# Gate and up projections: seven block products in place of eight for three of eight pairs of K tiles

## The chip, the cores and the metric

The kernel runs on one core of one Trainium2 chip. The metric is the device time of one execution in microseconds (us). TensorE is called PE below, VectorE DVE, ScalarE ACT, GpSimd POOL and SyncE SP; PEld is TensorE's loading of the stationary operand.

## The reference

The program is a two-layer encoder trunk over 256 tokens of width 2048, all in float32. Each layer computes

```
h = x + W_out [ attention | convolution | spatial gating ](RMSNorm(x))
x = h + ( silu(n @ W_gate) * (n @ W_up) ) @ W_down        with n = RMSNorm(h)
```

and a last RMSNorm follows. `W_gate` and `W_up` are 2048 x 5632 in each layer, and `W_down` is 5632 x 2048. The change is in `n @ W_gate` and `n @ W_up`; what the kernel must return is the same.

## The kernel before, in words

**Three matmuls for one float32 product.** Every operand of a large matmul is held as a high part (rounded to the type that TensorE reads in one pass, `F32R`) and a low part (what is left). A product is then xh·wh + xh·wl + xl·wh, three matmuls that add into one PSUM bank (`three`, L300, and `three_tok`, L316). The activations' parts are made once. The weights' parts are made as they arrive.

**The weight stream.** The host packs all weights, in the order of use, into chunks of 128 x 2048 float32 (1 MB). The class `Weights` (L60) loads them through SP's queue into three `raw` buffers, and splits each chunk into two halves of 1024 columns: ACT casts to the high part `wh` (L96), and DVE subtracts to get the low part `wl` (L97). There are four buffers for split halves. `take` (L106) hands out the next columns, and keeps the splitting three halves ahead. When both halves of a chunk are split, its raw buffer is released and the next load is issued (L102 to L104).

**Gate and up.** The 5632 hidden features go in eleven groups of 512 (`G`). For one group, PE goes through the 16 K tiles (128 input channels each) in the order of `UP_ORDER`. For each K tile there are two token tiles of 128 tokens and two weight blocks (gate and up), so four products of 128 x 128 by 128 x 512, twelve matmuls (`token_products`, L308, called at L644). The sums stand in four PSUM banks: `ag` (gate) and `au` (up) for both token tiles, out of a pool `ps` of five banks. Two further pools, `pm` (two banks) and `pmc` (one), serve small results. After the 16 K tiles, ACT applies silu to `ag` (L655), DVE multiplies with `au` (L657), and the result `ht` waits. In the middle of the next group, after four K tiles (L647), PE transposes `ht` eight times (L232) into `pt`, and ACT and DVE make the high and low parts of the hidden activations (`hilo`, L190 and L191).

**Down.** The eleven groups are taken in parts of four, four and three (`PARTS`). After a part's gate and up, its share of the down projection runs: for each of four column blocks of 512, the part's K tiles add up in two banks `ad`, and DVE adds them to the residual stream `xt` (L327). The hidden parts live in tiles `hm0` to `hm7`.

**Who sets the order.** The kernel is written for a planner. The order of the program text gives priorities; at build time the planner simulates the engines and gives each engine a fixed list, in which a later instruction can stand ahead of an earlier one that was not ready in the simulation. It also assigns buffers out of each pool as they come free. On the chip each engine works through its list in order and waits on semaphores.

**Before gate and up.** The output projection (`OUT_ORDER`, L608 to L622) finishes the column blocks 2, 3, 0, 1 in this order. As each is finished, `feed_group` (L238) transposes the block of `xt`, and ACT and DVE write the scaled high and low parts into `xs` (L221 and L222). The order of K tiles in gate and up begins with 8 for this reason.

Of the kernel before, what the change touches and what calls it, by code (L numbers as in the profile page):

```python
# [17 lines left out]
P = 128  # L18
# [8 lines left out]
HALO = TAPS // 2  # L27
EPS = 1e-6
NEG = -3.0e38
SCALE = 1.0 / math.sqrt(128.0)  # L30
CH = 2048
HC = CH // 2

OFF_Q, OFF_K, OFF_V, OFF_CA, OFF_CG, OFF_U, OFF_VS = 0, 1024, 1280, 1536, 2048, 2560, 3072
MIX_FIRST = [0, 1, 2, 3, 4, 5, 6, 7, 12, 13, 14, 15]
# [10 lines left out]

UP_ORDER = list(range(8, KT)) + list(range(8))

PARTS = [(0, 4), (4, 4), (8, 3)]

# [9 lines left out]
class Weights:  # L60

    AHEAD = 3

    def __init__(self, nc, w, raw_pool, split_pool):
        self.nc, self.w = nc, w
        self.n = w.shape[0]
        self.raw_pool, self.split_pool = raw_pool, split_pool
        self.raw, self.parts = {}, {}  # L70
        self.loaded = self.split_done = 0
        self.cur, self.off = -1, HC

    def load(self, pieces=1, after_first=None):
# [10 lines left out]
        self.loaded += 1  # L85

    def split(self, pieces=1):
        i = self.split_done
        if i >= 2 * self.n:
            return  # L90
        r = self.raw[i // 2][:, i % 2 * HC:(i % 2 + 1) * HC]
        h = self.split_pool.tile([P, HC], F32R, tag="wh", name=f"wh{i}")
        lo = self.split_pool.tile([P, HC], F32R, tag="wl", name=f"wl{i}")
        for k in range(pieces):
            c = slice(k * HC // pieces, (k + 1) * HC // pieces)
# [4 lines left out]
        self.parts[i] = (h, lo)  # L100
        self.split_done += 1
        if i % 2 == 1:  # L102
            self.raw.pop(i // 2)
            self.load()  # L104

    def take(self, n):  # L106
        if self.off == HC:
            self.parts.pop(self.cur, None)
            self.cur += 1
            self.off = 0  # L110
            while self.split_done <= min(self.cur + self.AHEAD, 2 * self.n - 1):
                self.split()
        h, lo = self.parts[self.cur]
        c = slice(self.off, self.off + n)
        self.off += n
        return h[:, c], lo[:, c]


@with_exitstack
def encoder_kernel(  # L120
# [19 lines left out]

    W = Weights(nc, w, raw_pool, split_pool)

# [13 lines left out]
    xt = [acts.tile([P, D], F32, name=f"xt{t}") for t in range(2)]  # L156
    xs = [acts.tile([P, 2 * S], F32R, name=f"xs{k}") for k in range(KT)]

# [37 lines left out]
    class Sums:  # L196


        def __init__(self, name, engine=nc.vector):
            self.engine = engine  # L200
            self.acc = tmp.tile([P, S], F32, tag="sqacc", name=f"sqacc_{name}")
            self.n = 0

        def add(self, k):
            if self.n == 0:
                nc.scalar.activation(self.acc, x[k], AF.Square)
            else:
                q = tmp.tile([P, S], F32, tag="spb", name="sq", bufs=4)
# [29 lines left out]
    def feed_group(n, gcol):  # L238
        for i in range(0, 4, 2):
            pt = transposed(xt, 4 * n + i)  # L240
            for j in range(2):
                feed(4 * n + i + j, gcol, pt[:, j, :])

    class TokenSums:

# [4 lines left out]
        def add(self, n):  # L250
            for t in range(2):
                q = tmp.tile([P, G], F32, tag="pts", name="sq")
# [63 lines left out]
    def three_tok(a, xh, xl, wh, wl, first, last):  # L316
        nc.tensor.matmul(a, xh, wh, start=first, stop=False)  # L317
        nc.tensor.matmul(a, xh, wl, start=False, stop=False)  # L318
        nc.tensor.matmul(a, xl, wh, start=False, stop=last)  # L319

    def token_acc(name):
        return [ps.tile([P, G], F32, tag="ps", name=f"{name}{t}") for t in range(2)]
# [35 lines left out]
    def rope(t):  # L358

        sw = tmp.tile([32, 2, S], F32, tag="sw", name="sw", bufs=1)  # L360
        nc.vector.stream_shuffle(sw, t[:32], SWAP)
        cos = tb[:32, T_COS:T_COS + S].unsqueeze(1).to_broadcast([32, 2, S])
        sin = tb[:32, T_SIN:T_SIN + S].unsqueeze(1).to_broadcast([32, 2, S])
        nc.vector.tensor_tensor(out=sw, in0=sw, in1=sin, op=ALU.mult)
        nc.vector.tensor_tensor(out=t[:32], in0=t[:32], in1=cos, op=ALU.mult)
        nc.vector.tensor_tensor(out=t[:32], in0=t[:32], in1=sw, op=ALU.add)


    def scores(l, p, t, qT, kT, sc):
        g = p // 2  # L370
        pS = pm.tile([P, 2, S], F32, tag="pm", name="pS")
        for hh in range(2):
# [3 lines left out]
        sm = tmp.tile([P, 2, S + 1], F32, tag="sm", name="sm", bufs=4)  # L376
        mask = tb[:, T_MASK + t * S:T_MASK + (t + 1) * S].unsqueeze(1).to_broadcast([P, 2, S])
# [20 lines left out]
    def mix_values(p, t, sm, v):  # L398
        g = p // 2
        pT = pm.tile([P, 4, P], F32, tag="pm", name="pT")  # L400
        for hh in range(2):
            for kt in range(2):
                nc.tensor.transpose(
                    pT[:, 2 * hh + kt, :], sm[:, hh, kt * P:(kt + 1) * P], ident
                )
        pts = tmp.tile([P, 4, P], F32, tag="pts", name="pts")
        nc.scalar.copy(out=pts, in_=pT)
# [69 lines left out]
    def sgu_v(l, t, acc, rc, lr):  # L477

        vg = tmp.tile([P, 512], F32, tag="vg", name="vg")
        nc.scalar.activation(vg, acc, AF.Gelu, scale=rc[:, t:t + 1])  # L480
# [47 lines left out]
    for l in range(DEPTH):  # L528
# [5 lines left out]
                 for c in range(4)]  # L534
        ys = [tmp.tile([P, S], F32, tag="cy", name=f"cy{c}", bufs=4) for c in range(4)]
        for c in range(4):
# [31 lines left out]

        kT = tmp.tile([P, 2, S], F32, tag="kT", name="kT", bufs=1)
# [4 lines left out]
        v = tmp.tile([P, 2, S], F32, tag="v", name="v", bufs=1)  # L574
        va = proj_tok(256)
# [5 lines left out]
        for p in range(4):  # L581
            qT = tmp.tile([P, 2, S], F32, tag="qT", name="qT", bufs=2)
# [16 lines left out]
        vn = [sgu_v(l, t, va[t], rc, lr) for t in range(2)]  # L599
        spb = [tmp.tile([P, S], F32, tag="spb", name=f"spb{h}", bufs=4) for h in range(4)]  # L600
        sgu_mix(vn, lr, spb)
# [4 lines left out]
        sums = TokenSums(f"f{l}")  # L606
        accs = {}
        for n, kts, begin, end, complete in OUT_ORDER:  # L608
# [11 lines left out]
            if complete:  # L620
                feed_group(n, C_G2 + l * KT)
                sums.add(n)  # L622
# [16 lines left out]
        for g0, gn in PARTS:  # L639
            for j in range(gn):  # L640
                ag, au = token_acc("ag"), token_acc("au")
                for i, k in enumerate(UP_ORDER):
                    wh, wl = W.take(2 * G)
                    token_products(  # L644
                        [ag, au], lambda p: xs_part(k, p), wh, wl, i == 0, i == KT - 1
                    )
                    if i == 3 and pending:  # L647
                        hidden_parts(*pending)
                        pending = None
                if j == 0:  # L650
                    new_hm(2 * gn, f"h{l}_{g0}_")
                ht = []
                for t in range(2):
                    z = tmp.tile([P, G], F32, tag="qT", name="sgate")
                    nc.scalar.activation(z, ag[t], AF.Silu, scale=rf[:, t:t + 1])  # L655
                    h = tmp.tile([P, G], F32, tag="sm", bufs=4, name="ht")
                    nc.vector.scalar_tensor_tensor(  # L657
                        out=h, in0=au[t], scalar=rf[:, t:t + 1], in1=z,
                        op0=ALU.mult, op1=ALU.mult,
                    )  # L660
                    ht.append(h)
                pending = (ht, 4 * j)
# [44 lines left out]
def _pack_weights(w_in, w_out, w_gate, w_up, w_down):  # L707
# [17 lines left out]
    for l in range(DEPTH):  # L725
# [18 lines left out]
        for g0, gn in PARTS:  # L744
            for j in range(g0, g0 + gn):
                c = slice(j * G, (j + 1) * G)
                put(np.concatenate([w_gate[l][:, c], w_up[l][:, c]], axis=1), UP_ORDER, 0, 2 * G)
            for n in range(NG):
# [68 lines left out]
```

## Time and profile before

| | |
|---|---|
| median of 3 runs | 2030.5 us (2030.2 to 2031.33) |
| the profiled execution's own time | 2030.33 us |
| its span | 2028.5 us |
| busy in the span | PE 99%, PEld 85%, DVE 59%, ACT 46%, POOL 2% |
| mean granted TensorE clock | 0.998 |
| HBM read | 377.21 MB, 187 GB/s over the span |

The profile is one execution on the chip. Busy time is the time that an engine spent in instructions. A PE busy share is not a share of its peak, since matmuls overlap: the start of one matmul to the start of the next is the time that it costs. The same holds for DVE and ACT, where the next instruction can start shortly before the listed end of the one before.

### The profile page before, as it was taken

To read this page: it belongs to the slowest core of one execution; us is meant where nothing else is said; L and a number is where in the kernel's file an instruction comes from. 1 tells how busy PE (TensorE), PEld (TensorE's weight loads), DVE (VectorE), ACT (ScalarE), POOL (GpSimd) and SP (SyncE) were. 2 spreads that over 40 slices of the span, in tenths; PEclk is the share of its full clock that TensorE was granted. 3 is DMA by queue.
4 is the path that set the end of the run, shared out by engine and by line. 5 is a ranking of instruction groups with operands and counts; after the bars stand their busy time and mean duration, and the time that the engine had idled before them with its cause. 6 is when DMAs were issued, how large, how long until landed. Compare 5 with 4: busy or idle time off the path is not lost.

```text
span 2028.5 us, 25066 instructions
## 1 busy us (share of the span) xinstructions
PE 2009.2 (99%) x10196; PEld 1717.5 (85%) x10196; DVE 1188.3 (59%) x1450; ACT 933.2 (46%) x1163; POOL 31.5 (2%) x49
## 2 busy tenths in 40 slices
PE   8999999999999999999999999999999999999997
PEld 8999888888888888888899998888888888888886
DVE  8997664445445455455579975644555445545454
ACT  6357554444344443344544664544443444434443
POOL 2000000000000000000000000000000000000000
PEclk9999999999999999999999999999999999999999
DMA  7554555555555555555455445555555555555553
GB/s 266 207 208 146 195 180 188 193 194 191 187 194 186 193 194 188 190 185 202 172 185 187 147 158 198 183 188 189 193 193 192 187 188 190 194 195 189 186 188 122
DMA packets 55701, 380.94 MB, mean 188 GB/s; under 512 B 6304, under 2 KB 8608, under 8 KB 10272
## 3 DMA queue, kind: packets, MB, share of 16 engines
q1 hardware_dynamic: 55584, 379.33, 52.5%
q8 instruction: 80, 1.31, 0.3%
q14 instruction: 37, 0.30, 0.0%
HBM read 377.21 MB, written 2.10 MB: 187 GB/s over the span
## 4 chain that ended last, share of the span: by engine, by line
PE 98%; ACT 0%; DVE 0%; DMA 0%; issue 0%; SPq 0%; POOLq 0%; DVEq 0%; ACTq 0%
PE ag L317 8%; PE ag L318 8%; PE ag L319 8%; PE au L319 8%; PE au L317 8%; PE au L318 8%; PE ad L319 8%; PE ad L317 8%; PE ad L318 8%; PE acc L302 4%; PE acc L303 4%; PE acc L301 4%; PE ao L317 3%; PE ao L319 3%; PE ao L318 3%; PE pt L232 1%
## 5 line engine op out<-in xcount | busy, mean ns | idle before, releaser
L97 DVE TENSOR_TENSOR wl<-raw,wh 128x1024 fp32r<-128x1024 f32 (+1 forms) x706 | 861.7, 1222 | 796.8 <-ACT wh L96 790.6
L96 ACT CAST wh<-raw 128x1024 fp32r<-128x1024 f32 (+1 forms) x706 | 741.2, 1051 | 1019.3 <-PE au L319 535.6
L317 PE MATMUL ag<-wh,xs 128*128 128x512 f32 x704 | 275.5, 391 | 0.0
L318 PE MATMUL ag<-wl,xs 128*128 128x512 f32 x704 | 274.2, 390 | 0.0
L317 PE MATMUL au<-wh,xs 128*128 128x512 f32 x704 | 274.1, 389 | 0.0
L319 PE MATMUL ag<-wh,xs 128*128 128x512 f32 x704 | 274.1, 389 | 0.0
L319 PE MATMUL au<-wh,xs 128*128 128x512 f32 x704 | 274.0, 389 | 0.0
L318 PE MATMUL au<-wl,xs 128*128 128x512 f32 x704 | 273.9, 389 | 0.0
L318 PE MATMUL ad<-wl,h 128*128 128x512 f32 x704 | 273.2, 390 | 0.0
L319 PE MATMUL ad<-wh,h 128*128 128x512 f32 x704 | 272.0, 389 | 0.0
L317 PE MATMUL ad<-wh,h 128*128 128x512 f32 x704 | 270.9, 390 | 0.0
L301 PE MATMUL acc<-xs,wh 128*128 128x256 f32 x704 | 196.4, 286 | 7.1 <-ACT xs L221 7.1
L302 PE MATMUL acc<-xs,wh 128*128 128x256 f32 x704 | 200.3, 286 | 0.3 <-DVE xs L222 0.3
L303 PE MATMUL acc<-xs,wl 128*128 128x256 f32 x704 | 199.5, 286 | 0.0
L319 PEld LDWEIGHTS ag<-wh,xs 128*128 128x128 f32 x704 | 132.2, 188 | 27.6
L318 PEld LDWEIGHTS ad<-wl,h 128*128 128x128 f32 x704 | 132.2, 188 | 27.6
L317 PEld LDWEIGHTS au<-wh,xs 128*128 128x128 f32 x704 | 132.2, 188 | 27.6
L319 PEld LDWEIGHTS au<-wh,xs 128*128 128x128 f32 x704 | 132.2, 188 | 27.5
L318 PEld LDWEIGHTS au<-wl,xs 128*128 128x128 f32 x704 | 132.2, 188 | 27.5
L319 PEld LDWEIGHTS ad<-wh,h 128*128 128x128 f32 x704 | 132.2, 188 | 27.4
L317 PEld LDWEIGHTS ag<-wh,xs 128*128 128x128 f32 x704 | 132.2, 188 | 26.8
L318 PEld LDWEIGHTS ag<-wl,xs 128*128 128x128 f32 x704 | 132.2, 188 | 26.8
(146 smaller groups left out, 1970.7 us busy)
## 6 DMA issues: line engine op xcount, KB each, us to landing
raw<-w SPq DMA_DIRECT2D x349, 1024.0 KB, 4.8
x<-xT SPq DMA_DIRECT2D x16, 128.0 KB, 5.2
raw<-w SPq DMA_DIRECT2D x4, 512.0 KB, 6.8
lr<-lrow SPq DMA_DIRECT2D x2, 1024.0 KB, 6.0
xt<-xN SPq DMA_DIRECT2D x2, 1024.0 KB, 5.1
out<-xt SPq DMA_DIRECT2D x2, 640.0 KB, 4.4
raw<-w SPq DMA_DIRECT2D x4, 256.0 KB, 4.0
gf<-lrow SPq DMA_DIRECT2D x1, 1024.0 KB, 7.3
```

What stands on the lines that cost most here:

```text
L96: self.nc.scalar.copy(out=h[:, c], in_=r[:, c])
L97: self.nc.vector.tensor_tensor(out=lo[:, c], in0=r[:, c], in1=h[:, c].bitcast(F32), op=ALU.subtract)
L232: nc.tensor.transpose(pt[:, i, t * P:(t + 1) * P], src[t][:, (i0 + i) * P:(i0 + i + 1) * P], ident,)
L301: nc.tensor.matmul(acc, wh, xh, start=first, stop=False)
L302: nc.tensor.matmul(acc, wh, xl, start=False, stop=False)
L303: nc.tensor.matmul(acc, wl, xh, start=False, stop=last)
L317: nc.tensor.matmul(a, xh, wh, start=first, stop=False)
L318: nc.tensor.matmul(a, xh, wl, start=False, stop=False)
L319: nc.tensor.matmul(a, xl, wh, start=False, stop=last)
```

## The change

Two neighbouring K tiles, two token tiles and the pair gate/up make a 2 x 2 by 2 x 2 block product, eight block products of three matmuls each. For three of the eight pairs ("S" in `UP_PAIRS`) it is done with seven products of sums and differences (a Strassen-Winograd scheme); the other five ("P") keep eight. The order of the pairs is P S P S P S P P.

- All pairs add into seven running sums `m1` to `m7`, one PSUM bank each: five of `ps`, the one of `pmc` (`m5`) and one of the two of `pm` (`m4`). In a P pair the second token tile and the difference of the token tiles take the place of the two token tiles, so that the sums come out in the same form.
- After the last S pair (`LAST_S`) one ACT copy and two DVE additions take `m1`, `m6` and `m7`; after the last pair one ACT copy and five DVE operations make the gate and up sums. Silu and the product work on these in SBUF.
- The weight sums of an S pair are made on the chip: its chunk gives four split units (1024, 512, 1024 and 1024 columns) in place of two, and DVE makes three additions (1024, 512 and 512 columns) into two tiles that use the buffers `hm6` and `hm7`. `AHEAD` goes from 3 to 4, and the split buffers from 4 to 5.
- The parts are of three, three, three and two groups, so that `hm6` and `hm7` are free of hidden activations.
- `feed_sums` replaces `feed_group` in the output projection: it also makes the high and low parts of the sums and differences of the activations, which stay in SBUF for the layer.
- The small temporary tiles of many tags share one pool tag `u` of 16 buffers.

```diff
-UP_ORDER = list(range(8, KT)) + list(range(8))
-PARTS = [(0, 4), (4, 4), (8, 3)]
+UP_PAIRS = [(4, "P"), (5, "S"), (6, "P"), (7, "S"), (0, "P"), (1, "S"), (2, "P"), (3, "P")]
+KIND = dict(UP_PAIRS)
+LAST_S = max(i for i, (_, kind) in enumerate(UP_PAIRS) if kind == "S")
+PARTS = [(0, 3), (3, 3), (6, 3), (9, 2)]
...
-    AHEAD = 3
+    AHEAD = 4
...
+    def source(self, i, u):
+        raw = self.raw[i]
+        if self.kinds[i] != "S":
+            return raw[:, u * HC:(u + 1) * HC]
+        if u == 0:
+            return raw[:, HC:]
+        if u == 1:
+            return raw[:, 512:HC]
+        if u == 2:
+            f = self.sum_tile(0)
+            self.add(
+                f.rearrange("p (a b) -> p a b", a=2),
+                raw[:, 0:512].unsqueeze(1).to_broadcast([P, 2, 512]),
+                raw[:, 512:512 + HC].rearrange("p (a b) -> p a b", a=2),
+            )
+            self.sums[i] = f
+            return f
+        g = self.sum_tile(1)
+        self.add(g[:, :512], self.sums.pop(i)[:, 512:], raw[:, 512:HC])
+        self.add(g[:, 512:], g[:, :512], raw[:, HC + 512:])
+        return g
...
-    split_pool = ctx.enter_context(tc.tile_pool(name="split", bufs=4))
+    split_pool = ctx.enter_context(tc.tile_pool(name="split", bufs=5))
...
+    def sum_tile(i):
+        return hpool.tile([P, HC], F32, tag=f"hm{6 + i}", name=f"fs{i}")
...
+    def feed_sums(n, gcol, forms):
+        for i in (2 * n, 2 * n + 1):
+            pt = transposed(xt, 2 * i)
+            a = unit2("xg")
+            for j in range(2):
+                g = cs[:, gcol + 2 * i + j:gcol + 2 * i + j + 1]
+                nc.scalar.activation(a[:, j, :], pt[:, j, :], AF.Copy, scale=g)
+            hilo(xp[i][:, :, :S], xp[i][:, :, S:], a)
+            x11, x21 = a[:, 0, :P], a[:, 0, P:]
+            x12, x22 = a[:, 1, :P], a[:, 1, P:]
+            f = unit("gf")[:, :4 * P].rearrange("p (a b) -> p a b", a=4)
+            if KIND[i] == "S":
+                sub(f[:, 0], x21, x22)
+                sub(f[:, 1], f[:, 0], x11)
+                sub(f[:, 2], x11, x21)
+                nc.vector.tensor_tensor(out=f[:, 3], in0=x12, in1=f[:, 1], op=ALU.add)
+                hi = unit(f"gh{i}", F32R)[:, :4 * P].rearrange("p (a b) -> p a b", a=4)
+                lo = unit(f"gl{i}", F32R)[:, :4 * P].rearrange("p (a b) -> p a b", a=4)
+                hilo(hi, lo, f)
+                forms[i] = [(hi[:, q], lo[:, q]) for q in range(4)]
+            else:
+                sub(f[:, :2], a[:, :, :P], a[:, :, P:])
+                d = unit(f"gd{i}", F32R)[:, :4 * P].rearrange("p (a b) -> p a b", a=4)
+                hilo(d[:, :2], d[:, 2:], f[:, :2])
+                forms[i] = [(d[:, q], d[:, 2 + q]) for q in range(2)]
...
+    def gate_up(forms, pending):
+        plan = []
+        for i, kind in UP_PAIRS:
+            if kind == "S":
+                order = [
+                    (1, x_form(2 * i, 0)), (2, x_form(2 * i + 1, 0)), (3, forms[i][3]),
+                    (7, forms[i][2]), (5, forms[i][0]), (6, forms[i][1]),
+                    (4, x_form(2 * i + 1, 1)),
+                ]
+                plan.append([(m, x, 0) for m, x in order])
+            else:
+                one = []
+                for j in range(2):
+                    x1, x2 = x_form(2 * i + j, 0), x_form(2 * i + j, 1)
+                    one += [(2, x1, 0), (3, forms[i][j], 1), (5, x2, 2), (4, x2, 3)]
+                plan.append(one)
+        ...
+        for m in (1, 7, 6, 2, 3):
+            bank[m] = ps.tile([P, G], F32, tag="ps", name=f"m{m}")
+        bank[5] = pm.tile([P, G], F32, tag="pmc", name="m5", bufs=1)
+        bank[4] = pm.tile([P, G], F32, tag="pm", name="m4", bufs=2)
+        ...
+        for b, block in enumerate(plan):
+            if b == 1 and pending:
+                hidden_parts(*pending)
+            ...
+            if b == LAST_S:
+                nc.scalar.copy(out=s1, in_=bank[1])
+                nc.vector.tensor_tensor(out=u2, in0=bank[6], in1=s1, op=ALU.add)
+                nc.vector.tensor_tensor(out=u3, in0=bank[7], in1=u2, op=ALU.add)
+        s3, c22 = unit("s3")[:, :G], unit("c22")[:, :G]
+        nc.vector.tensor_tensor(out=s1, in0=bank[2], in1=s1, op=ALU.add)
+        nc.scalar.copy(out=s3, in_=bank[3])
+        nc.vector.tensor_tensor(out=s3, in0=bank[5], in1=s3, op=ALU.add)
+        sub(c22, bank[5], u3)
+        nc.vector.tensor_tensor(out=u3, in0=bank[4], in1=u3, op=ALU.add)
+        sub(s3, s3, u2)
+        return (s1, u3), (s3, c22)
```

## Rows read from the trace of the kernel before

**Rows 1.** The page's busy times: us, share of the span, instructions of each engine.
```profile
PE 2009.2 (99%) x10196; PEld 1717.5 (85%) x10196; DVE 1188.3 (59%) x1450; ACT 933.2 (46%) x1163; POOL 31.5 (2%) x49
```

**Rows 2.** The page's chain that ended last, shares of the span by engine.
```profile
PE 98%; ACT 0%; DVE 0%; DMA 0%; issue 0%; SPq 0%; POOLq 0%; DVEq 0%; ACTq 0%
```

**Rows 3.** Stretches: length, busy us per engine (instructions), granted clock, DMA share, GB/s.
```profile
60.00:100.00 40.00, 40.00 (x335) 40.00 (x335) 38.78 (x71) 16.23 (x19) 1.52 (x1) 1.00 0.57 211
205.00:282.00 77.00, 77.00 (x353) 64.04 (x352) 47.50 (x59) 41.13 (x61) 1.51 (x1) 1.00 0.56 200
338.86:383.32 44.46, 44.46 (x202) 36.88 (x201) 22.12 (x20) 19.11 (x20) 0.00 (x0) 1.00 0.53 191
478.00:546.00 68.00, 68.00 (x304) 56.34 (x303) 35.19 (x33) 27.04 (x27) 0.00 (x0) 1.00 0.52 190
```

**Rows 4.** The chain in order of time, one group of gate/up: start us, length.
```profile
338.86 0.87 PE pt L232 x8
383.32 0.87 PE pt L232 x8
```

**Rows 5.** PE's timeline around eight transposes: start us, length, instruction.
```profile
427.60 1.03 PE L232 MATMUL pt<-tb,ht 128*128 128x128 f32 x8
428.39 0.49 PE L317 MATMUL ag<-wh,xs 128*128 128x512 f32 x1
428.71 0.40 PE L318 MATMUL ag<-wl,xs 128*128 128x512 f32 x1
```

**Rows 6.** DVE's timeline where instructions follow back to back: start us, length.
```profile
74.51 1.21 DVE L97 TENSOR_TENSOR wl<-raw,wh 128x1024 fp32r<-128x1024 f32 x1
75.65 0.86 DVE L439 SCALAR_TENSOR_TENSOR cy<-cpad,cs,cy 128x256 f32<-128x256 f32 x2
76.44 0.67 DVE L364 TENSOR_TENSOR sw<-sw,tb 32x512 f32<-32x512 f32 x1
77.04 0.67 DVE L365 TENSOR_TENSOR kT<-kT,tb 32x512 f32<-32x512 f32 x1
...
385.57 1.28 DVE L191 TENSOR_TENSOR h<-pt,h 128x512 fp32r<-128x512 f32 x2
...
416.43 1.40 DVE L657 SCALAR_TENSOR_TENSOR ht<-au,c_b,sgate 128x512 f32<-128x512 f32 x2
```

**Rows 7.** ACT's and DVE's timelines in gate/up, steady state: [idle before <- releaser].
```profile
389.72 1.05 ACT L96 CAST wh<-raw 128x1024 fp32r<-128x1024 f32 x1 [1.67 <-PE au L319]
392.44 1.05 ACT L96 CAST wh<-raw 128x1024 fp32r<-128x1024 f32 x1 [1.67 <-PE au L319]
...
390.80 1.23 DVE L97 TENSOR_TENSOR wl<-raw,wh 128x1024 fp32r<-128x1024 f32 x1 [1.50 <-ACT wh L96]
```

**Rows 8.** Groups of instructions by line: busy us, mean ns | idle before.
```profile
L97 DVE TENSOR_TENSOR wl<-raw,wh 128x1024 fp32r<-128x1024 f32 x702 | 858.9, 1225 | 790.6 <-ACT wh L96 784.4
L655 ACT ACTIVATE sgate<-ag,c_b 128x512 f32<-128x512 f32 x44 | 30.1, 684 | 8.9 <-PE ag L319 8.9
L190 ACT CAST h<-pt 128x512 fp32r<-128x512 f32 x44 | 23.5, 586 | 0.0
```

**Rows 9.** Waits (total us, times, longest) and the loads (KB, median us to landing).
```profile
ACT wh L96 <- DMA raw<-w: 4.4, 5, 1.9
...
SPq L81 <- DVE wl L97: 1682.9, 326, 8.5
...
raw<-w SPq DMA_DIRECT2D x349, 1024.0 KB, 4.8
```

**Rows 10.** PE's timeline where gate/up begins, banks still held by the output projection.
```profile
283.86 0.39 PE L317 MATMUL ag<-wh,xs 128*128 128x512 f32 x1
...
284.54 0.39 PE L317 MATMUL ag<-wh,xs 128*128 128x512 f32 x1
...
288.06 0.48 PE L317 MATMUL au<-wh,xs 128*128 128x512 f32 x1
```

More of the change, by code (lines that the diff above doesn't have):

```diff
@@ L28 @@
 EPS = 1e-6
+NU = 16
 NEG = -3.0e38
@@ L60, with __init__ @@
 class Weights:
-    AHEAD = 3
-    def __init__(self, nc, w, raw_pool, split_pool):
+    AHEAD = 4
+    def __init__(self, nc, w, kinds, raw_pool, split_pool, sum_tile):
         self.nc, self.w = nc, w
         self.n = w.shape[0]
-        self.raw_pool, self.split_pool = raw_pool, split_pool
-        self.raw, self.parts = {}, {}
+        assert len(kinds) == self.n
+        self.raw_pool, self.split_pool, self.sum_tile = raw_pool, split_pool, sum_tile
+        self.units = [
+            (i, u) for i in range(self.n) for u in range(4 if kinds[i] == "S" else 2)
+        ]
+        self.kinds = kinds
+        self.raw, self.sums, self.parts = {}, {}, {}
         self.loaded = self.split_done = 0
-        self.cur, self.off = -1, HC
+        self.cur, self.off, self.width = -1, 0, 0
     def load(self, pieces=1, after_first=None):
@@ L116, in take, with chunk_kinds @@
         return h[:, c], lo[:, c]
+def chunk_kinds():
+    kinds = []
+    for _ in range(DEPTH):
+        kinds += ["P"] * (MIX_COLS * KT // CH + D * KT // CH)
+        for _, gn in PARTS:
+            kinds += [kind for _, kind in UP_PAIRS] * gn
+            kinds += ["P"] * (4 * gn * D // CH)
+    return kinds
 @with_exitstack
@@ L200, in __init__ @@
             self.engine = engine
-            self.acc = tmp.tile([P, S], F32, tag="sqacc", name=f"sqacc_{name}")
+            self.acc = unit(f"sqacc_{name}")[:, :S]
             self.n = 0
@@ L207, in add @@
             else:
-                q = tmp.tile([P, S], F32, tag="spb", name="sq", bufs=4)
+                q = unit("sq")[:, :S]
                 nc.scalar.activation(q, x[k], AF.Square)
@@ L251, in add @@
             for t in range(2):
-                q = tmp.tile([P, G], F32, tag="pts", name="sq")
+                q = unit("sq")[:, :G]
                 nc.scalar.activation(
@@ L319, in three_tok, with x_form, product @@
         nc.tensor.matmul(a, xl, wh, start=False, stop=last)
+    def x_form(k, t):
+        c = slice(t * P, (t + 1) * P)
+        return xs_part(k, 0)[:, c], xs_part(k, 1)[:, c]
+    def gate_up(forms, pending):
[6 more added lines that the diff above has]
+                    (4, x_form(2 * i + 1, 1)),
+                ]
+                plan.append([(m, x, 0) for m, x in order])
[5 more added lines that the diff above has]
+                plan.append(one)
+        seq = [m for block in plan for m, _, _ in block]
+        left = {m: seq.count(m) for m in set(seq)}
+        bank = {}
+        for m in (1, 7, 6, 2, 3):
+            bank[m] = ps.tile([P, G], F32, tag="ps", name=f"m{m}")
+        bank[5] = pm.tile([P, G], F32, tag="pmc", name="m5", bufs=1)
+        bank[4] = pm.tile([P, G], F32, tag="pm", name="m4", bufs=2)
+        begun = set()
+        def product(m, x, wh, wl):
+            left[m] -= 1
+            three_tok(bank[m], x[0], x[1], wh, wl, m not in begun, left[m] == 0)
+            begun.add(m)
+        s1, u2, u3 = unit("s1")[:, :G], unit("u2")[:, :G], unit("u3")[:, :G]
+        for b, block in enumerate(plan):
+            if b == 1 and pending:
+                hidden_parts(*pending)
+            if UP_PAIRS[b][1] == "S":
+                for m, x, _ in block:
+                    product(m, x, *W.take(G))
+            else:
+                for j in range(2):
+                    gh, gl = W.take(G)
+                    uh, ul = W.take(G)
+                    for m, x, q in block[4 * j:4 * j + 4]:
+                        if q in (0, 3):
+                            product(m, x, gh, gl)
+                        else:
+                            product(m, x, uh, ul)
+            if b == LAST_S:
[10 more added lines that the diff above has]
+        return (s1, u3), (s3, c22)
@@ L534, in encoder_kernel @@
                  for c in range(4)]
-        ys = [tmp.tile([P, S], F32, tag="cy", name=f"cy{c}", bufs=4) for c in range(4)]
+        cy = [unit2(f"cy{i}") for i in range(2)]
+        ys = [cy[c // 2][:, c % 2, :] for c in range(4)]
         for c in range(4):
@@ L599, in encoder_kernel @@
         vn = [sgu_v(l, t, va[t], rc, lr) for t in range(2)]
-        spb = [tmp.tile([P, S], F32, tag="spb", name=f"spb{h}", bufs=4) for h in range(4)]
+        sp2 = [unit2(f"spb{i}") for i in range(2)]
+        spb = [sp2[h // 2][:, h % 2, :] for h in range(4)]
         sgu_mix(vn, lr, spb)
@@ L746, in _pack_weights @@
                 c = slice(j * G, (j + 1) * G)
-                put(np.concatenate([w_gate[l][:, c], w_up[l][:, c]], axis=1), UP_ORDER, 0, 2 * G)
+                gu = np.concatenate([w_gate[l][:, c], w_up[l][:, c]], axis=1)
+                for i, kind in UP_PAIRS:
+                    pair = (2 * i, 2 * i + 1)
+                    if kind == "S":
+                        put(gu, pair, G, G)
+                        put(gu, pair, 0, G)
+                    else:
+                        put(gu, pair, 0, 2 * G)
             for n in range(NG):
```

78 lines of the change are left out of this document (40 added, 38 removed).

## The prediction

> **What bounds the kernel now.** I read the page's busy times first, then the chain of waits, then the stretches, and last the timelines of one group of 512 features. PE is busy 99% of the span, DVE 59% [rows 1], and the chain that ends last is 98% PE [rows 2]. So PE's own work sets the time. The stretch of one group in gate and up shows it without a gap: 44.46 us, PE busy in all of it, DVE in 22.12, ACT in 19.11, the granted clock at full rate, 2.4 GHz [rows 3]. From one block of transposes to the next is 44.46 us [rows 4]. The eight transposes take 0.79 us and the first matmul behind them is 0.09 late (0.32 to the next start) [rows 5], 0.88 together. The other 43.58 us are 192 matmuls: 0.227 us each.
>
> The reader should see two more things. In the stretch from 60 to 100 us DVE is busy 38.78 of 40.00 us, and PE still shows no idle time and 335 matmuls [rows 3]: a nearly full DVE alone does not hold PE up, though there much of DVE's work is of low priority. And where gate and up begins, the second gate product of the first K tile starts at 283.86, but the up product beside it only at 288.06, with products of later K tiles put ahead (from 284.54), and no gap [rows 10]: where a bank is not free, the planner fills PE with other products.
>
> **What is removed.** In a group, three S pairs need 21 matmuls in place of 24: nine of 192 go, 9 x 0.227 = 2.04 us. Eleven groups in two layers: 22 x 2.04 = 44.9 us. P pairs, the down projection and all else keep their matmul counts. A group's PE time becomes 183 x 0.227 + 0.88 = 42.4 us. No S product is another shape, so I keep 0.227 for each.
>
> **What DVE gets.** DVE's costs are start to start. A 128 x 1024 subtraction: 74.51 to 75.65, 1.14 us; 128 x 512: 76.44 to 77.04, 0.60; from PSUM, two in 1.28 of which the last lasts 0.68, so 0.60 too; the silu product, two in 1.40 with 0.74 for the last, 0.66 [rows 6]. No row shows the weight additions; they are two-input float32 operations of the same sizes, so I take 1.14 and 0.60, and as the high end the listed 1.225 [rows 8] and 0.68.
> - P pair: two splits, 2.28. S pair: four splits (3 x 1.14 + 0.60 = 4.02) and three additions (1.14 + 2 x 0.60 = 2.34), 6.36.
> - Five P, three S: 11.4 + 19.1 = 30.5. Combining the seven sums: seven operations of 0.60, 4.2. Silu products 2 x 0.66 and hidden low parts 2 x 0.60: 2.5. Together 37.2 us of PE's 42.4, 88%.
>
> Before it was 16 x 1.14 + 2.5 = 20.7, so DVE gets 16.5 us more in each group. All of it lies beside PE if it comes in time; 5.2 us per group are left over.
>
> The Trainium skill (VectorE: DVE Perf Modes, The DRAIN you can't avoid) says that the next DVE operation does not start until the pipe of the one before has emptied. By that each would cost its listed length, and the group would need about 40.8 us, 96%, with less room but the same sum. The rows differ from it: 74.51 + 1.21 is past 75.65 [rows 6].
>
> **Does it come in time?** With five split buffers, a buffer that PE frees is filled again while PE works on the next four units: 4.8 us where these are one S pair (21 x 0.227), 10.9 where they are two P pairs. A refill is a cast, and a subtraction that starts 1.08 after the cast does (389.72 to 390.80) and lasts 1.23: 2.3 us [rows 7]. S pairs ask for more DVE time (6.4) than they give PE work (4.8), P pairs give 5.45 and ask 2.3: P S is 8.6 of 10.2, in balance. The tight place is the start of a group. Behind the last group DVE has four combinations (2.4) and the silu products (1.3); then come the last two units of the first S pair (2.3 each), the hidden parts (1.2) and the first half of the next P pair (1.1), 10.6 us. PE needs the last of these after P, transposes and S, 11.1 us. It fits with 0.5 us to spare, and with 2.8 if the additions, which wait for no split buffer, run in the slack of the two P pairs before. I take no loss here; if a late order puts one more split in front, a group loses up to 1.1.
>
> **Banks.** Seven of eight are held. `m1`, `m6`, `m7` come free after the last S pair, two P pairs (10.9 us) before the group's end. `m2` and `m3` get their last matmuls nine and six matmuls before the end (2.0 and 1.4 us), and DVE's and ACT's reads take 0.6 each. `m5` is read twice after its last matmul (0.7 before the end), so it is free about 0.8 us into the next group and wanted 1.4 in; `m4` has a second `pm` bank. If one is late, PE has products for other banks [rows 10]. From nothing to 0.6 per group; I take 0.1, 2.2 us in all, near the row without a gap. One `pm` bank is left for both blocks of transposes, so four and four will stand apart: the 0.09 restart [rows 5] a second time, 22 x 0.09 = 2.0 us.
>
> **ACT** gets four and a half more unit casts per group (1.05 each [rows 7]) and two copies of 0.59 [rows 8]: 19.1 + 5.9 = 25 of 42.4 us, hidden by PE. An S unit's addition, cast and subtraction hang on each other, so DVE may stand for 1.08 us at a derived unit unless the planner puts something between; six of these per group are 6.5 us, 1.3 more than the 5.2 left over. That is the price if the cover is gone.
>
> **Weights.** The same bytes come in, one chunk per 5.3 us in place of 5.56. A landing takes 4.8 us; SP waits for splits (1682.9 us), and casts waited for data only 4.4 us [rows 9]. A raw buffer of an S pair is held for four units in place of two; two chunks are still on the way, some 10 us. Cost zero.
>
> **Output projection.** `feed_sums` has, per layer, 8 operations of 0.60, and for three S pairs four small ones (no row; at most the 0.60 of 512 columns, at least nothing, I take 0.3) and one of 0.60, for five P pairs two of about 0.4: about 14 us of DVE against 16 x 0.4 = 6.4 before, beside 29.5 us in which DVE stood idle there [rows 3]. Zero, at most 2 us a layer if a form is late for its pair.
>
> **One part more.** Per layer eight residual additions more (0.60 each), beside 33 idle DVE us in 68 of down [rows 3]. The part of two groups leaves four K tiles (24 x 0.227 = 5.4 us) to finish its last group: combinations 2.4, silu 0.7 [rows 8], products 1.3, so 4.4; with a split in the way 5.5. I take 0.5 per layer, 1 us.
>
> **Sum.** 2030.3 (the profiled execution; its span is 1.8 less, and the median 0.2 more) - 44.9 + 2.2 + 2.0 + 1.0 = 1990.6; I say 1990.5 us.
>
> **Rivals.**
> 1. *A late buffer in each group.* DVE is one split late at the tight place, or a bank comes free one DVE operation late: 1.14 us in each of 22 groups, 25 us: 1990.5 + 25 = 2015. For it: 0.5 us to spare in the worst order, and seven banks in turn. Against it: the planner's filling [rows 10].
> 2. *DVE becomes the bound, and the kernel is slower.* Place: the S pairs. DVE stands for the cast at each derived unit (6 x 1.08 = 6.5), and for ACT's or its own results in the combining chain (about 3.0, five steps of 0.6). The group then needs 37.2 + 9.5 = 46.7 against 44.46 before: 22 x 2.24 = +49, about 2080 us. It decides from 5.2 us of such waits per group, and the kernel is slower than before from 44.46 - 37.2 = 7.3. For it: DVE waited 784 us for casts in the trace [rows 8]. Against it: those were waits with nothing else to do, since the casts themselves waited for PE [rows 7]; and at 97% DVE the stretch from 60 to 100 us has no such gaps. The Trainium skill (TensorE: Matmul & The Clock Gate, Architectural detail) says that ACT and DVE are strict first-in first-out, by which a badly placed wait would hold all behind it; the trace of before shows no such case that cost PE time.
>
> **How the numbers follow.** The forecast 75%, rival 1 14%, rival 2 11%. The likeliest case's own range is 1985 (no losses but the sum's 44.9) to 2003 (0.6 per group at the banks, 11 us, and 2 more). The range for 8 in 10 reaches from 1984 to 2018, which takes in rival 1's middle and leaves out its tail and rival 2. A difference under 0.2% (4 us) is no change that a measurement of this kernel can tell: faster 0.86 (the forecast, and rival 1 without its tail), same 0.03, slower 0.11.
>
> **What would show it.** After: 22 group stretches of 42.5 us with 183 matmuls at 0.227 and two sets of four transposes; DVE busy near 90% of them by its listed lengths, and few of its waits for casts left; no PE gaps at group seams. Rival 1 would show PE gaps of about 1 us behind a low part or a combination, once per group. Rival 2 would show DVE waits for casts of over 5 us per group, and PE waiting for low parts of S units. The forecast is wrong if PE's matmul pitch changes, or if the down stretches grow by more than 1 us a part.

## The result and the profile after

The changed kernel takes 2042.8 us (median of 4 runs, 2042.0 to 2043.2), the kernel before 2030.4 beside it: ratio 1.006, 95% interval 1.0042 to 1.0077. It is slower by 0.6%, where 1990.5 us and faster were forecast.

The page of the profiled execution after: span, busy times, chain by engine.
```profile
span 2040.3 us, 25520 instructions
...
PE 2003.2 (98%) x9998; PEld 1685.3 (83%) x9998; DVE 1563.5 (77%) x1984; ACT 1066.2 (52%) x1373; POOL 28.2 (1%) x49
...
PE 96%; ACT 2%; DVE 1%; issue 0%; DMA 0%; SPq 0%; POOLq 0%; DVEq 0%
```
Against [rows 1, 2]: PE has 198 matmuls less and is busy only 6.0 us less, where 198 x 0.227 = 44.9 were to go. DVE rose as planned, and PE still makes up the chain, though 3% of it now belongs to ACT and DVE.

Stretches after: one group of gate and up from transposes to transposes, and 40 us of the down projection; columns as in [rows 3].
```profile
546.12:589.07 42.95, 42.95 (x193) 35.11 (x192) 37.84 (x44) 24.42 (x29) 0.00 (x0) 1.00 0.54 196
446.00:486.00 40.00, 40.00 (x173) 32.16 (x172) 22.64 (x23) 15.74 (x15) 0.00 (x0) 1.00 0.53 186
```
The group went from 44.46 [rows 4] to 42.95, with DVE busy 37.84 and ACT 24.42: close to the 42.5, 37.2 and 25 of the prediction. It is 0.55 us more than the 42.4 of the prediction's sum, some 12 us in 22 groups; the rest of the loss lies outside the groups. The next table has, for each stage, the time from its first matmul to the first of the next stage, both layers together, worked out from the matmul starts of each trace (the columns from the third on are runs of the next section).

| stage, us | before | after | tiles moved | + banks | + units | own buffers |
|---|---|---|---|---|---|---|
| mixing | 356.1 | 379.6 | 380.8 | 379.8 | 378.8 | 355.6 |
| output projection | 192.6 | 188.9 | 185.8 | 184.8 | 184.0 | 193.4 |
| gate and up | 976.0 | 952.9 | 955.2 | 942.1 | 929.1 | 928.2 |
| down | 486.9 | 501.8 | 488.7 | 488.6 | 488.6 | 488.5 |

After against before: mixing +23.5, output -3.7 (part of its attention work now runs ahead of it), gate and up -23.1, down +14.9; together +11.6. Three things stand out in the trace.

**A longer matmul.** The pitch of a stream of matmuls is the time from the start of one to the start of the next. PE's timeline in the down projection after: start us, listed length.
```profile
469.67 0.39 PE L409 MATMUL ad<-wh,h 128*128 128x512 f32 x1
469.90 0.40 PE L410 MATMUL ad<-wl,h 128*128 128x512 f32 x1
470.14 0.39 PE L411 MATMUL ad<-wh,h 128*128 128x512 f32 x1
470.37 0.40 PE L409 MATMUL ad<-wh,h 128*128 128x512 f32 x1
```
Three matmuls from 469.67 to 470.37: 0.233 us each, where before it was 0.227. A whole part, 288 matmuls, takes 68.03 us; without the 0.88 for its transposes that is 0.233 too. Nothing waits, the listed lengths barely differ, and PE reads as fully busy: only the starts show it. In the output projection it is the same, in gate and up 0.230 on the mean.

**A wait for a bank, and half clock.** PE's timeline where gate and up begins after, then the same place as stretches.
```profile
305.53 1.21 PE L293 MATMUL pt<-tb,xt 128*128 128x128 f32 x8
310.27 0.63 PE L409 MATMUL m<-wh,xs 128*128 128x512 f32 x1 [3.53 <-ACT xg L316]
310.70 0.63 PE L410 MATMUL m<-wl,xs 128*128 128x512 f32 x1
311.12 0.63 PE L411 MATMUL m<-wh,xs 128*128 128x512 f32 x1
```
```profile
305.00:310.00 5.00, 1.74 (x11) 1.13 (x10) 3.16 (x8) 4.01 (x11) 0.00 (x0) 1.00 0.45 187
310.00:314.00 4.00, 3.73 (x9) 2.94 (x10) 3.00 (x5) 3.97 (x9) 0.00 (x0) 0.57 0.00 0
314.00:318.00 4.00, 4.00 (x19) 3.25 (x18) 3.58 (x8) 4.00 (x8) 0.70 (x1) 1.00 0.16 29
```
Two blocks of transposes hold both `pm` banks until ACT has copied them (`xg`), `m4` needs one of the two, and PE stands for 3.53 us. Then the granted clock falls to 0.57 on the mean of 4 us: matmuls start 0.43 apart, as at 1.2 GHz, and from 314 us at full rate again. The first part of gate and up is 7.4 us longer than the second in each layer (before 1.8).

**Attention's products back to back.** PE's waits over the whole execution, after and then before, those of the mixing stage and of the first product of the output projection among them (total us, times, longest).
```profile
PE po L573 <- ACT pts L569: 10.0, 8, 2.6
PE m L409 <- ACT xg L316: 7.1, 2, 3.5
PE acc L393 <- ACT xs L282: 6.8, 2, 5.4
PE ao L409 <- ACT vg L642: 1.7, 2, 0.8
```
```profile
PE acc L301 <- ACT xs L221: 7.1, 2, 5.2
PE ao L317 <- ACT mix L190: 0.4, 1, 0.4
```
The worst place after, on PE and then on ACT:
```profile
192.52 0.60 PE L565 MATMUL pT<-tb,sm 128*128 128x128 f32 x4
195.74 1.16 PE L573 MATMUL po<-pts,v 128*128 128x128 f32 x8 [2.62 <-ACT pts L569]
197.74 0.72 PE L409 MATMUL ao<-wh,mix 128*128 128x512 f32 x1 [0.84 <-ACT vg L642]
198.26 0.63 PE L410 MATMUL ao<-wl,mix 128*128 128x512 f32 x1
198.68 0.63 PE L411 MATMUL ao<-wh,mix 128*128 128x512 f32 x1
```
```profile
191.77 1.28 ACT L632 ACT_TABLE_LOAD   x1
193.06 1.09 ACT L632 ACTIVATE cy<-cy,cs 128x256 f32<-128x256 f32 x2
194.06 0.35 ACT L251 CAST mix<-po 128x256 fp32r<-128x256 f32 x1
194.31 0.40 ACT L251 CAST mix<-cy 128x256 fp32r<-128x256 f32 x1
194.62 0.60 ACT L632 ACTIVATE cy<-cy,cs 128x256 f32<-128x256 f32 x1
195.12 0.57 ACT L569 COPY pts<-pT 128x512 f32<-128x512 f32 x1
```
The planner put the last transposes (`pT`) and value products (`po`) next to each other, with no matmul between them, and the convolution's norm in the midst. `po` needs ACT's copy of `pT`, and the copy stands on ACT behind a table load, three silus and two casts. The first output product is late in its turn, and again the clock falls (0.43 apart from 198.26). The prediction named the rule of the Trainium skill (TensorE: Matmul & The Clock Gate, Architectural detail) that ACT works strictly in order; these rows agree with it, by 2.62 us.

Before, thirty matmuls of a projection stand between these transposes and the value products that follow, and PE does not wait:
```profile
177.90 0.60 PE L403 MATMUL pT<-tb,sm 128*128 128x128 f32 x4
...
181.94 1.05 PE L411 MATMUL po<-pts,v 128*128 128x128 f32 x8
```

### The profile page after: what moved, and what is told of

It is laid out like the page before. It is cut to its first block, busy times and chain, and to the rows that moved or that the text cites. A ratio compares the mean times of both kernels' runs of the same rounds, so it can differ in the third digit from the quotient of the medians.

```text
span 2040.3 us, 25520 instructions
## 1 busy us (share of the span) xinstructions
PE 2003.2 (98%) x9998; PEld 1685.3 (83%) x9998; DVE 1563.5 (77%) x1984; ACT 1066.2 (52%) x1373; POOL 28.2 (1%) x49
## 4 chain that ended last, share of the span: by engine, by line
PE 96%; ACT 2%; DVE 1%; issue 0%; DMA 0%; SPq 0%; POOLq 0%; DVEq 0%
PE m L409 15%; PE m L411 15%; PE m L410 15%; PE ad L410 8%; PE ad L409 8%; PE ad L411 8%; PE acc L394 4%; PE acc L395 4%; PE acc L393 4%; PE ao L409 3%; PE ao L410 3%; PE ao L411 3%; PE pt L293 1%; PE acct L513 1%; PE acct L514 1%; PE acct L515 1%
## 5 line engine op out<-in xcount | busy, mean ns | idle before, releaser
L137 DVE TENSOR_TENSOR wl<-raw,wh 128x1024 fp32r<-128x1024 f32 (+1 forms) x706 | 817.7, 1169 | 333.7 <-ACT wh L136 328.9
L410 PE MATMUL m<-wl,xs 128*128 128x512 f32 x858 | 336.5, 392 | 0.0
L411 PE MATMUL m<-wh,xs 128*128 128x512 f32 x858 | 335.2, 393 | 0.0
L409 PE MATMUL m<-wh,xs 128*128 128x512 f32 x858 | 312.1, 393 | 7.1 <-ACT xg L316 7.1
L136 ACT CAST wh<-fs 128x1024 fp32r<-128x1024 f32 x132 | 138.4, 1050 | 164.4 <-PE m L411 127.4
L137 DVE TENSOR_TENSOR wl<-fs,wh 128x1024 fp32r<-128x1024 f32 x132 | 160.0, 1222 | 54.4 <-ACT wh L136 54.2
L409 PEld LDWEIGHTS m<-wh,xs 128*128 128x128 f32 x858 | 162.0, 189 | 42.3 <-ACT xg L316 7.5
L410 PEld LDWEIGHTS m<-wl,xs 128*128 128x128 f32 x858 | 161.8, 189 | 36.2
L411 PEld LDWEIGHTS m<-wh,xs 128*128 128x128 f32 x858 | 161.8, 189 | 35.2
L411 PEld LDWEIGHTS ad<-wh,h 128*128 128x128 f32 x704 | 132.2, 188 | 31.7
L409 PEld LDWEIGHTS ad<-wh,h 128*128 128x128 f32 x704 | 132.3, 188 | 31.3
L393 PEld LDWEIGHTS acc<-xs,wh 128*128 128x128 f32 x704 | 134.2, 194 | 7.3 <-ACT xs L282 7.1
L394 PEld LDWEIGHTS acc<-xs,wh 128*128 128x128 f32 x704 | 136.3, 194 | 0.5 <-DVE xs L283 0.3
L395 PEld LDWEIGHTS acc<-xs,wl 128*128 128x128 f32 x704 | 135.9, 193 | 0.2
```

The costliest lines, as they stand in the source:

```text
L137: self.nc.vector.tensor_tensor(out=lo[:, c], in0=r[:, c], in1=h[:, c].bitcast(F32), op=ALU.subtract)
L393: nc.tensor.matmul(acc, wh, xh, start=first, stop=False)
L394: nc.tensor.matmul(acc, wh, xl, start=False, stop=False)
L395: nc.tensor.matmul(acc, wl, xh, start=False, stop=last)
```

## The experiments

Theory: three separate causes, each a side effect. (A) The matmul's pitch depends on where the stationary operand lies in SBUF. (B) `m4`'s bank makes PE wait at the start of gate and up. (C) Sharing the temporaries' buffers changes the planner's order in the mixing stage. The addresses below are the program's memory layout, which follows from the pools' tile sizes; no trace shows them. Before, weights, `xs` and hidden tiles all begin 96 bytes past a multiple of 256. After, weights and `xs` still do, hidden tiles lie at 224, and the shared units, 2080 bytes apart, at all eight multiples of 32.

**The hidden tiles moved back (after).** Rival: the pitch follows the drops of the clock.
```
- mean = tmp.tile([P, S], F32, tag="cz", name="mean", bufs=1)
+ mean = tmp.tile([P, S + 32], F32, tag="cz", name="mean", bufs=1)[:, :S]
```


> The changed kernel with 128 bytes per partition more in front of the hidden tiles, nothing else: they begin at 196448 in place of 196320, so at the same distance from a multiple of 256 bytes as the weight tiles and as in the kernel before. Theory A (the matmul pitch depends on where the stationary operand lies): the 2880 matmuls of the output and down projections go from about 0.233 back to 0.227 us each, and the time falls by about 18 us, from 2043 to about 2025; gate and up unchanged. Theory B (the pitch follows what the clock did before: the drops to 1.2 GHz at about 195 and 308 us remain): pitch and time unchanged, 2043 within 3 us.

Measured: 2025.6 us (10 runs, 2023.6 to 2029.2; the profiled one is the longest), ratio to before 0.9979 (0.997 to 0.9989). 17.2 us less for 128 bytes of padding. PE in the down projection of that run:
```profile
469.83 0.39 PE L409 MATMUL ad<-wh,h 128*128 128x512 f32 x1
470.06 0.39 PE L410 MATMUL ad<-wl,h 128*128 128x512 f32 x1
470.29 0.39 PE L411 MATMUL ad<-wh,h 128*128 128x512 f32 x1
470.51 0.39 PE L409 MATMUL ad<-wh,h 128*128 128x512 f32 x1
```
Three in 0.68 us, 0.227 again, and 66.2 us for the part, with the clock's drops still there. The rival falls. In the trace PE, ACT and DVE go through the same instructions in the same order as in the changed kernel, and so they do in the next three runs against the kernel before: what these four runs changed is the place alone.

**The same padding in the kernel before**, the same line edited.

> The kernel before with the same 128 bytes in front of the hidden tiles, nothing else: they move from the weight tiles' distance from a multiple of 256 bytes to that which the changed kernel has. Theory A (place of the stationary operand): output and down projections, 2880 matmuls, go from 0.227 to about 0.233 us each, so about 2030 + 18 = 2048 us; the rest unchanged. Theory B (clock drops set the pitch, and this kernel has none): no change, 2030 within 3 us.

Measured: 2047.6 us, ratio 1.0084 (1.0069 to 1.0099), +17.3. The slow pitch is made at will in a kernel without the change, at a mean clock of 0.998.

**Everything in the kernel before moved together.**
```
- warm = consts.tile([P, 1], F32, name="warm")
+ warm = consts.tile([P, 33], F32, name="warm")[:, :1]
```


> The kernel before with 128 bytes more ahead of all its tiles but the first constants, so that weights, activations and hidden tiles all lie 224 bytes past a multiple of 256, none moved against another. If the pitch depends on where the stationary operand lies against the moving one: 0.227 us as before, 2030 within 3 us. If it depends on the stationary operand's own place (224 slow, 96 fast, as in the runs that moved the hidden tiles alone): 0.233 for all 7,300 matmuls of 512 columns, about 45 us more, 2075.

Measured: 2029.9 us, ratio 0.9997 (0.9988 to 1.0007). In these runs what counts is the distance between stationary and moving operand, not the place of either.

**64 bytes in place of 128 (before)**: `S + 16` in the line of the first experiment.

> The kernel before with 64 bytes in front of the hidden tiles, where the earlier run had 128 (2047.6 us). If any distance between stationary and moving operand that is no multiple of 256 costs the same: 2047 to 2049. If the cost grows with the distance: about half, 2039. If only the distance mod 64 or 128 mattered, the run with 128 would not have been slower, so no change is not expected.

Measured: 2049.3 us, ratio 1.0093 (1.0076 to 1.011). 64 bytes cost as much as 128 (1.7 us more), so the cost does not shrink with the distance. PE's timeline here, and then with everything moved together:
```profile
489.71 0.40 PE L318 MATMUL ad<-wl,h 128*128 128x512 f32 x1
489.95 0.39 PE L319 MATMUL ad<-wh,h 128*128 128x512 f32 x1
490.18 0.40 PE L317 MATMUL ad<-wh,h 128*128 128x512 f32 x1
490.42 0.39 PE L318 MATMUL ad<-wl,h 128*128 128x512 f32 x1
```
```profile
489.63 0.39 PE L318 MATMUL ad<-wl,h 128*128 128x512 f32 x1
489.86 0.39 PE L319 MATMUL ad<-wh,h 128*128 128x512 f32 x1
490.09 0.39 PE L317 MATMUL ad<-wh,h 128*128 128x512 f32 x1
490.31 0.39 PE L318 MATMUL ad<-wl,h 128*128 128x512 f32 x1
```
Three matmuls in 0.71 us (0.23 and 0.24 in turn) and in 0.68.

**The banks of m1 and m4 exchanged**, on top of the moved tiles.
```
- for m in (1, 7, 6, 2, 3):
+ for m in (4, 7, 6, 2, 3):
- bank[4] = pm.tile([P, G], F32, tag="pm", name="m4", bufs=2)
+ bank[1] = pm.tile([P, G], F32, tag="pm", name="m1", bufs=2)
```


> As the run with the hidden tiles moved, and the banks of the running sums m1 and m4 exchanged: m4, which the first block needs four times, no longer lies in the pool of two that the transposes of the last sums of x hold at the start of gate and up; m1, which only S blocks use, does. Theory (the wait of 3.5 us for a bank and the half clock behind it, at about 306 to 314 us, come from m4's bank): this wait and the drop go, 5 to 7 us per layer, 10 to 14 us less than the run with only the tiles moved. Rival (the sums of x are late themselves, or m1's wait takes the place): less than 3 us in all.

Measured: 2014.4 us, ratio 0.9922 (0.9906 to 0.9939): 11.1 less. The start of gate and up in the run with only the tiles moved, and then in this one:
```profile
300.00:320.00 20.00, 16.46 (x65) 13.01 (x64) 16.55 (x28) 18.42 (x37) 0.69 (x1) 0.83 0.29 106
```
```profile
300.00:320.00 20.00, 20.00 (x93) 16.39 (x92) 17.82 (x27) 16.98 (x33) 0.00 (x0) 1.00 0.55 200
```
The wait and the drop are gone.

**The units 2304 bytes apart**, on top of that, so that the forms of x begin at 96 too (space from the unused DMA scratch).
```
- return tmp.tile([P, 514], dtype, tag="u", name=name, bufs=NU)
+ return tmp.tile([P, 576], dtype, tag="u", name=name, bufs=NU)[:, :514]
- nc = _bacc.Bacc(..., num_devices=1)
+ nc = _bacc.Bacc(..., num_devices=1, dynamic_dma_scratch_size=4096)
```


> As the run with tiles moved and the banks of m1 and m4 exchanged (2014.4 us), and the shared units 2304 bytes apart in place of 2080, so that all sixteen, those that hold the forms of x among them, begin 96 bytes past a multiple of 256 like the weights. Theory A (place of the stationary operand): the pitch of the matmuls in gate and up goes from about 0.230 to 0.227 us on the mean, 4026 x 0.003 = about 12 us less: 2002. Rival (the forms are slow because of their own shape or because PE waits for their low parts): no change, 2014 within 3 us.

Measured: 2000.0 us, ratio 0.9851 (0.9834 to 0.9867): 14.4 less, 13 of them in gate and up, where PE's instructions keep their order. The starts show where the time was lost: in the changed kernel, 0.232 us from one matmul on a form to the next, and 0.227 on `xs` with no form among the five matmuls before and behind; beside a form, `xs` pays too. Here it is 0.227 throughout.

**The lookahead alone (before).**
```
- AHEAD = 3
+ AHEAD = 4
- split_pool = ctx.enter_context(tc.tile_pool(name="split", bufs=4))
+ split_pool = ctx.enter_context(tc.tile_pool(name="split", bufs=5))
```


> The kernel before with the fifth split buffer and the lookahead of four units (the hidden tiles still at 96 bytes past a multiple of 256), nothing else of the change. If the deeper lookahead is what moves the mixing stage's order, that stage grows by about 10 us per layer, as in the changed kernel (180.8 to 192.3 in the first layer), and the time is about 2050. If the shared pool of 16 units does it, this run stays within 4 us of 2030.

Measured: 2030.1 us, ratio 1.0 (0.999 to 1.0009). The lookahead alone costs nothing, though by the trace it changes the order of instructions too.

**The shared pool and the lookahead (before)**: on top of the last edit, the change's `unit` and `unit2` (16 buffers) in place of the mixing stage's tags, with the hidden tiles kept at 96. Two of its lines:
```
- sm = tmp.tile([P, 2, S + 1], F32, tag="sm", name="sm", bufs=4)
+ sm = unit("sm").rearrange("p (a b) -> p a b", a=2)
...
- kT = tmp.tile([P, 2, S], F32, tag="kT", name="kT", bufs=1)
+ kT = unit2("kT")
```


> The kernel before with the shared pool of 16 units for the mixing stage's temporaries and with the fifth split buffer and lookahead of four; gate and up, down and the addresses mod 256 of the matmul operands as before. Theory (the shared pool together with the lookahead changes the planner's order in the mixing stage: transposes and value products back to back, the convolution's norm among them): mixing and output stages together grow by 8 to 12 us per layer, 2047 to 2054 in all. Rival (the mixing stage's loss comes from something else of the change, the pairs of x tiles or the weight units): 2030 within 4 us.

Measured: 2045.8 us, ratio 1.0077 (1.0062 to 1.0092); mixing and output +15.5 us in two layers. PE's waits of this run:
```profile
PE po L418 <- ACT pts L414: 10.0, 8, 2.6
PE acc L308 <- ACT xs L228: 7.1, 2, 5.2
PE ao L324 <- ACT vg L487: 0.8, 1, 0.8
```
The changed kernel's waits of 10.0 us are here, in a kernel with the old gate and up. +15.2 is less than the 17 to 24 that I gave; the place was right.

**The shared pool alone (before)**: the same without the edit of the lookahead.

> The kernel before with the shared pool of 16 units alone, the lookahead of three and four split buffers kept, the hidden tiles at the weights' distance from a multiple of 256. The lookahead alone changed nothing (2030.1 us) and both together cost 15.2 us. If the pool alone does it, 2042 to 2048; if it takes both, 2030 within 4 us. In this kernel's instruction order the last two pairs of attention transposes and value products stand back to back, as with both, but the convolution's norm comes 150 matmuls later, ahead of the output projection only by its first part: so I expect about half, 2034 to 2042.

Measured: 2040.8 us, ratio 1.0051 (1.0036 to 1.0066). The pool alone costs 10.5 us, inside the 2034 to 2042 that were expected; the lookahead, free by itself, adds 5 on top of it. The waits for `pts` are shorter (with 4.1 us at the first output products, where before it was 0.4, they make 8.2 of the 10.5), and the granted clock stays at 1.00 from 100 to 240 us:
```profile
PE po L418 <- ACT pts L414: 4.1, 6, 0.7
```

**21 units in place of 16**, on the run with moved tiles and exchanged banks.

> As the run with tiles moved and the banks of m1 and m4 exchanged (2014.4 us), with 21 shared units in place of 16. If the mixing stage loses because its temporaries wait for a free unit: five more units give back some or all of it, up to 15 us, 1999 to 2010. If it loses by the order in which the instructions were put (which comes out the same with 21 units): mixing and output stages as before, 2014 within 4 us, the rest from forms that fall on other addresses.

Measured: 2015.8 us, ratio 0.9927 (0.9911 to 0.9944), and 10.0 us of waits for `pts` once more, with the same order of instructions on PE, ACT and DVE. The temporaries do not wait for a free unit; the order does the harm. Nor is it where attention's operands lie: with every unit at 96 the mixing stage still takes 378.8 us (the table's "+ units").

**Buffers of their own for the mixing stage**, with all operands at 96 and the banks exchanged. Forms of x lie in attention's buffers, which are free by then.
```
+ def own(tag, n, name, dtype=F32):
+     return tmp.tile([P, 512], dtype, tag=tag, name=name, bufs=n)
- d = unit(f"gd{i}", F32R)[:, :4 * P].rearrange(...)
+ d = own(*HOMES[i][0], f"gd{i}", F32R).rearrange(...)
- pts = unit("pts")[:, :4 * P].rearrange(...)
+ pts = own("pts", 2, "pts").rearrange(...)
...
```


> The changed kernel with hidden tiles and forms 96 bytes past a multiple of 256, m1 and m4's banks exchanged, and the mixing stage's temporaries in buffers of their own as in the kernel before (the forms of x lie in those buffers once they are free). Theory (shared pool): mixing and output stages come back to about 277 and 271 us per layer, 17 us less than with the pool; with the pitch at 0.227 in gate and up, 2014 - 17 - 12 = about 1985. Rival (the loss in the mixing stage stays, only the pitch falls): about 2002.

Measured: 1985.3 us (1984.5 to 1986.1), ratio 0.9777 (0.9763 to 0.9792): faster than both kernels, by 2.2% than the one before. One group of it:
```profile
525.90:568.27 42.37, 42.37 (x192) 35.17 (x191) 37.91 (x43) 24.34 (x29) 0.00 (x0) 1.00 0.54 198
```

**m4 back in pm, in that kernel.**

> The kernel with buffers of its own for the mixing stage and all operands at the same distance from a multiple of 256 (1985.3 us), with the banks of m1 and m4 as the changed kernel had them. If m4's bank alone causes the wait at the start of gate and up: 3.5 us of wait and some half clock in each layer come back, 11 us as between the two earlier runs, about 1996. Rival (the wait came from the late convolution norm of the shared pool's order, or from late forms of x): 1985 within 3 us.

Measured: 1988.8 us, ratio 0.9796 (0.9781 to 0.981). 3.5 us, neither 11 nor nothing. The place is
```profile
300.00:320.00 20.00, 19.78 (x87) 15.89 (x86) 17.78 (x21) 14.17 (x19) 0.00 (x0) 1.00 0.51 181
```
with one wait of 0.2 us, for a cast of weights and not for a bank, and no drop. With tiles moved only, the last eight transposes of `xt` run in one row at 304.93, the fifteen `m4` matmuls stand right behind them, and ACT has not copied either block. Here the transposes come four at a time:
```profile
289.32 0.60 PE L299 MATMUL pt<-tb,xt 128*128 128x128 f32 x4
291.14 0.60 PE L299 MATMUL pt<-tb,xt 128*128 128x128 f32 x4
292.98 0.60 PE L299 MATMUL pt<-tb,xt 128*128 128x128 f32 x4
```
Products for other banks stand between them and behind the last, and `m4` takes a bank that ACT has copied by then. So theory B was half of it: in these runs the bank becomes a wait of 3.5 us only in the order of the kernels with the shared pool. Either edit stops most of it, and of the 11.1 us at most 3.5 belong to the bank by itself. By the matmul starts, 2.0 of them lie in the first parts of gate and up and 0.8 in its other parts; 0.7 lie in the mixing stage, where both kernels have the same order on PE, and are no effect of the bank.

## Why the prediction was wrong

| | us |
|---|---|
| forecast | 1990.5 |
| losses counted that did not come | -5.2 |
| pitch in output and down projection (hidden tiles moved) | +17.2 |
| pitch in gate and up (units moved) | +14.4 |
| start of gate and up (banks exchanged) | +11.1 |
| order in the mixing stage (own buffers) | +14.7 |
| sum; measured 2042.8 | 2042.7 |

The last four rows are differences between successive runs, so the sum is bound to close; that each has its cause rests on the experiments. The last two are not independent of each other: in the kernel with buffers of its own the bank costs 3.5 us and not 11.1.

- *What is removed: right.* 44.9 us taken from the profiled 2030.3 give 1985.4; with the side effects gone the kernel takes 1985.3, or 1988.8 with `m4` in `pm` as the change has it.
- *What DVE gets, does it come in time, ACT: right.* DVE 37.8 to 37.9 and ACT 24.3 to 24.4 us in a group, no PE wait in it; 42.37 us where the first step said 42.4. Rivals 1 and 2 did not come: no wait per group, PE 96 to 99% of the chain. The 2.2 for banks, 2.0 for split transposes and 1.0 for the part more were hardly needed: within and between the groups PE waits for none of them. The two sets of transposes stand together in the kernel with buffers of its own; with `m4` back in `pm` they stand apart, and a group takes 42.45 us. To the section of the Trainium skill that the prediction set against [rows 6] (VectorE: DVE Perf Modes, The DRAIN you can't avoid) belongs one sentence more: an operation that is not held starts earlier. With it the rows do not differ: 1.14 us from start to start where 1.21 is listed.
- *"No S product is another shape, so I keep 0.227 for each": the step that failed most,* 31.6 us. It asked for shape and not for place, and took for every matmul that keeps its count that it keeps its time. The change moved the hidden tiles by 4480 bytes, 128 more than a multiple of 256, and the forms to all distances; the 2880 matmuls of the output and down projections went to 0.233 us, and the 4026 of gate and up to 0.230 on the mean. The prediction's own test for being wrong, the matmul's pitch and more than 1 us a down part, is what came: 68.03 us for a part of 288 against 288 x 0.227 + 0.88 = 66.3.
- *"Zero, at most 2 us a layer if a form is late for its pair": wrong,* 5.5 us a layer. I compared sums of DVE time, and the wait was for a bank behind ACT's copies; [rows 10] was read as filling without limit, but here products for other banks ran out and fifteen matmuls for `m4` were left.
- *The mixing stage had no term at all:* 14.7 us. The diff changes only buffers there, and I took a change of buffers for a change of nothing. In a kernel whose order a planner makes, it is a change of order; the lookahead too, though alone it cost nothing.

What stays open: by what rule of the planner a shared pool puts `pT` and `po` side by side. The runs show that it does, that its size is not the reason, and what it costs.

## What to carry to other kernels

When a change resizes or adds tiles, put stationary and moving operands back at the same distance from a multiple of 256 bytes, and read the starts of the untouched stages' matmuls: the pitch longer by 2.6% showed here in no wait and no busy share. A change of tags or buffer counts in a planned kernel is a change of order everywhere those tiles live, so every stage whose buffers move belongs in the sum. And a bank wanted first at a seam should not be of the pool that the stage before is still draining.

## What the hardware showed

- The pitch of 512-column matmuls (weights moving, activations stationary) was 0.227 us with stationary and moving operand equally far from a multiple of 256 bytes (96 and 96, 224 and 224), and 0.233 with 64 or 128 bytes between them. Why is not shown; no other size of matmul was tried, and no trace shows the addresses.
- PE's granted clock fell to the lower level (1.2 GHz) after a wait of 3.53 us, with matmuls 0.43 apart from 310.27 to 313.68, and from 198.26 after waits of 2.62 and 0.84 us, with eight value products between the two and one matmul behind. Waits of 0.7 us, and one of 1.49 us in the changed kernel's mixing stage, were not followed by a drop. The drop adds to the wait: eight pitches of 0.43 in place of 0.23, 1.6 us.
